# Seven block products of half size for most of w13 in a two-layer decoder trunk

## The chip, the cores and the metric

One core of a Trainium2 chip runs the whole trunk in one program. The metric is device time in microseconds of that core; lower is better. A run can be told from another of the same kernel to about 0.3%.

## What is computed

A trunk of two layers on 512 positions of width 1024, all in float32. Each layer is a feed-forward network, a token mixer and a second feed-forward network, each with a norm that is modulated by a conditioning vector, so there are four networks:

```python
def swiglu(h, w13, w2):
    a, b = jnp.split(h @ w13, 2, axis=-1)
    return (jax.nn.silu(a) * b) @ w2

x = x + 0.5 * g1[:, None] * swiglu(h, ff_w13[l, 0], ff_w2[l, 0])
```

`w13` is 1024 x 5632 (twice D_FF = 2816), `w2` is 2816 x 1024. The mixers (a gated convolution with latent attention in layer 0, sparse attention in layer 1) are not touched. The vectors of the modulation come from `silu(c) @ ada_w`.

## The kernel before

Features lie on the 128 partitions and the 512 positions in the columns. `x` and `h` are eight k-tiles of 128 x 512; `h` is held as a rounded high part and the rest (`hi`, `lo`), and so is each weight. `split` makes the two: ACT copies (L102), DVE subtracts (L103). A product is three matmul passes (`mm3`, L141 to L143): high by high, high by rest, rest by high.

`wunit` (L134) takes a raw weight tile from a ring (`wr`), loads 128-column units of up to eight k-tiles (512 KB) on SP's queue, and splits it into `wh` and `wl`. Each of the three rings has three tiles and one more inside a network (`more_weights`).

`ffn` goes over 22 column blocks `j` (D_FF / 128). A block multiplies `h` by the columns of `a` and of `b`, 24 matmuls of 512 columns each, and `gate` makes `silu(a) * b` and splits it into `g[j]`. The first blocks are made otherwise: in the first network `start` makes three while the first norm is taken; in the others `halves` makes two in two column halves (256 columns), beside the end of the norm before it. Then `proj_out` goes over the eight output blocks `d`: 22 k-tiles of `w2` times `g`, the residual added to `x` (L517), and squares for the next norm. Its last `d` is computed in two column halves, so that the norm of the first half starts early; `norm` hands in instructions through `inject`.

`background` loads `ada_w` in 128 tiles of 512 KB into the same `wr` ring and sums them on DVE (L300 to L304); `step` puts in so many tiles. It is called `st1` times per block `j` and `st2` times per unit of `proj_out`, in three of the networks.

The tile framework allocates buffers of a pool by tag: an instruction that needs a buffer waits for the last reader of the one before. Each engine, and each engine's DMA queue, works in order.

Of the kernel before, what the change touches and what calls it, by code (L numbers as in the profile page):

```python
# [1 line left out]

# [7 lines left out]
F32 = mybir.dt.float32  # L10
# [20 lines left out]
class Net:  # L31
# [6 lines left out]
    def __init__(self, tc, ctx, a):  # L38
# [70 lines left out]
    def wtile(self, kind, dt=R):  # L109

        counts = [n for _, n in self.wsets]
# [11 lines left out]
    def more_weights(self, ctx, name, n):  # L123

        self.wsets.append((ctx.enter_context(self.scratch(name)), n))
        ctx.callback(self.wsets.pop)
# [11 lines left out]
    def mm3(self, out, lhs, rhs, first, last):  # L138
        mm = self.nc.tensor.matmul
# [152 lines left out]
    def background(self, order):  # L292

        due = None
        for l, v in order:
            acc = self.t.tile([P, D], F32, name="acc", tag="acc", bufs=1)
            for k in range(KD):
# [7 lines left out]
                if k == 2 and due:  # L305
                    self.ada(*due)
# [94 lines left out]
    def modulate(self, l, n, d, bc, sl=slice(0, S)):  # L401
# [7 lines left out]
        sh = self.shift(l, n, d)  # L409
        nc.scalar.activation(hi[:, sl], u, AF.Identity, bias=sh)  # L410
# [44 lines left out]
    def ffn(self, l, which, nxt, st1, st2):  # L455
# [4 lines left out]
        ctx = ExitStack()  # L460
        g = []
        new = lambda pool, n: g.extend([[pool.tile([P, S], R, name=f"g{q}_{len(g) + k}") for q in range(2)]
                                        for k in range(n)])

        def gate(j, ab):
# [4 lines left out]
            self.split(gv, *g[j])  # L470

        with ctx:
            if l == 0 and which == 0:
                new(ctx.enter_context(self.scratch("ffa")), 11)
                ab = self.start(0, 0, w13)
                new(ctx.enter_context(self.scratch("ffb")), 11)
                self.more_weights(ctx, "ffw0", 1)
                done = 3
            else:
                new(ctx.enter_context(self.scratch(f"ff{l}{which}")), NJ)  # L480
                self.more_weights(ctx, f"ffw{l}{which}", 1)
# [790 lines left out]
```

## Time and profile before

| | |
|---|---|
| median of 3 runs | 2033.0 us (2030.45 to 2035.76) |
| profiled execution | 2030.4 us, span 2028.7 us |
| busy in the span | PE 1976.1, DVE 1133.6, ACT 767.5, POOL 227.2 us |
| mean granted clock of TensorE | 0.993 of 2.4 GHz |
| moved by DMA | 248.07 MB, mean 122 GB/s |

PE is the matmul engine, PEld its weight loads, which overlap. A matmul's end is modelled, so the distance between the starts of two matmuls says what one costs. Idle time of an engine that is not the bottleneck costs nothing.

### The profile page before, as it was taken

Reading aid. Unit: us, or ns where it says so; the run is one execution under the profiler, and the core shown is the slowest. Engines: PE = TensorE matmul, PEld = TensorE weight load, DVE = VectorE, ACT = ScalarE, POOL = GpSimd, SP = SyncE. Lnnn points to the kernel's source line nnn. Section 1 sums busy time; section 2 is a strip of 40 time slices with the busy share of each in tenths; the row PEclk is TensorE's granted clock in tenths of the full one; section 3 lists DMA queues with packets and bytes.
Section 4 is the critical chain, followed back from the end, with each engine's and each line's share of the span. In section 5 each row is a group of like instructions: output and inputs, shape, how many; then the busy total and the mean of one; then the engine's idle time right before and its main releaser. Section 6 shows DMA issues by size and latency. Waiting matters only on the chain.

```text
span 2028.7 us, 26175 instructions
## 1 busy us (share of the span) xinstructions
PE 1976.1 (97%) x10050; PEld 1669.5 (82%) x10050; DVE 1133.6 (56%) x1917; ACT 767.5 (38%) x1380; POOL 227.2 (11%) x468
## 2 busy tenths in 40 slices
PE   6999999998999999999999999999999999999998
PEld 5788878886889888888988888899788888888887
DVE  7746556358756666564545443356788763333332
ACT  3322222246734222222323222236777743322223
POOL 3000000024400000000100000020555410000000
PEclk8999999999999999999999999999999999999999
DMA  9646657332134566674436442333000134333331
GB/s 280 199 142 189 189 165 224 93 90 72 42 95 124 183 202 199 195 213 118 121 102 193 126 146 90 103 81 102 11 12 17 32 103 116 94 94 96 92 97 49
DMA packets 374562, 248.07 MB, mean 122 GB/s; under 512 B 23335, under 2 KB 356390, under 8 KB 374438
## 3 DMA queue, kind: packets, MB, share of 16 engines
q1 hardware_dynamic: 373568, 245.24, 41.0%
q8 instruction: 79, 1.29, 0.3%
q10 hardware_dynamic: 870, 1.16, 0.2%
q14 instruction: 45, 0.37, 0.1%
HBM read 244.28 MB, written 2.10 MB: 121 GB/s over the span
## 4 chain that ended last, share of the span: by engine, by line
PE 77%; DVE 8%; DMA 5%; ACT 4%; POOL 2%; issue 2%; DVEq 0%; SPq 0%; ACTq 0%; POOLq 0%
PE psA L141 17%; PE psA L143 16%; PE psA L142 16%; PE psY L141 7%; PE psY L143 7%; PE psY L142 7%; DMA wr<-in_ff_w 4%; PE psY L595 2%; DVE acc L236 1%; DVE wl L103 1%; ACT wh L102 1%; PE psA L561 1%; DVE pt L103 1%; ACT e L567 1%; PE psA L586 1%
## 5 line engine op out<-in xcount | busy, mean ns | idle before, releaser
L102 ACT ACTIVATE wh<-wr 128x1024 fp32r<-128x1024 f32 (+2 forms) x325 | 328.3, 1015 | 890.0 <-PE psA L142 317.3
L103 DVE TENSOR_TENSOR wl<-wr,wh 128x1024 fp32r<-128x1024 f32 (+2 forms) x325 | 381.5, 1179 | 414.2 <-ACT wh L102 408.7
L141 PE MATMUL psA<-h,wh 128*128 128x512 f32 (+1 forms) x1312 | 492.8, 379 | 7.5 <-ACT h L410 3.6
L143 PE MATMUL psA<-h,wl 128*128 128x512 f32 (+1 forms) x1312 | 490.2, 374 | 0.0
L142 PE MATMUL psA<-h,wh 128*128 128x512 f32 (+1 forms) x1312 | 487.9, 372 | 1.1 <-DVE h L411 1.0
L141 PEld LDWEIGHTS psA<-h,wh 128*128 128x128 f32 x1312 | 247.5, 189 | 48.4 <-ACT h L410 4.5
L142 PEld LDWEIGHTS psA<-h,wh 128*128 128x128 f32 x1312 | 247.9, 189 | 45.0 <-DVE h L411 2.4
L143 PEld LDWEIGHTS psA<-h,wl 128*128 128x128 f32 x1312 | 247.7, 189 | 43.7
L141 PE MATMUL psY<-h,wh 128*128 128x512 f32 (+2 forms) x568 | 209.0, 369 | 0.3 <-ACT wh L102 0.3
L143 PE MATMUL psY<-h,wl 128*128 128x512 f32 (+2 forms) x568 | 208.7, 367 | 0.0
L142 PE MATMUL psY<-h,wh 128*128 128x512 f32 (+2 forms) x568 | 207.7, 366 | 0.0
L141 PE MATMUL psA<-g,wh 128*128 128x512 f32 (+1 forms) x528 | 192.8, 365 | 0.0
L142 PE MATMUL psA<-g,wh 128*128 128x512 f32 (+1 forms) x528 | 191.9, 363 | 0.0
L143 PE MATMUL psA<-g,wl 128*128 128x512 f32 (+1 forms) x528 | 191.8, 363 | 0.0
L304 DVE SCALAR_TENSOR_TENSOR acc<-wr,cact,acc 128x1024 f32<-128x1024 f32 x112 | 143.7, 1283 | 59.6 <-DMA wr<-in_ada_w 58.2
L376 POOL TENSOR_SCALAR s<-s 128x2 int32<-128x2 int32 (+1 forms) x14 | 5.9, 420 | 1517.4 <-ACT s L375 1517.4
L142 PEld LDWEIGHTS psY<-h,wh 128*128 128x128 f32 (+1 forms) x568 | 106.1, 187 | 18.7
L141 PEld LDWEIGHTS psY<-h,wh 128*128 128x128 f32 (+1 forms) x568 | 106.1, 187 | 18.1 <-ACT wh L102 0.7
L143 PEld LDWEIGHTS psY<-h,wl 128*128 128x128 f32 (+1 forms) x568 | 106.0, 187 | 18.0
L143 PEld LDWEIGHTS psA<-g,wl 128*128 128x128 f32 x528 | 99.6, 189 | 16.0 <-DVE wl L103 0.6
L142 PEld LDWEIGHTS psA<-g,wh 128*128 128x128 f32 x528 | 99.7, 189 | 15.5
L141 PEld LDWEIGHTS psA<-g,wh 128*128 128x128 f32 x528 | 99.7, 189 | 15.4
(274 smaller groups left out, 2615.2 us busy)
## 6 DMA issues: line engine op xcount, KB each, us to landing
wr<-in_ff_w SPq DMA_DIRECT2D x234, 512.0 KB, 3.9
wr<-in_ada_w SPq DMA_DIRECT2D x128, 512.0 KB, 4.3
wr<-in_ff_w SPq DMA_DIRECT2D x40, 384.0 KB, 3.1
ar<-in_ada_w SPq DMA_DIRECT2D x16, 512.0 KB, 6.4
wr<-in_hy_w_in SPq DMA_DIRECT2D x15, 512.0 KB, 3.7
wr<-in_nsa_w_in SPq DMA_DIRECT2D x14, 512.0 KB, 3.7
wr<-in_hy_w_out SPq DMA_DIRECT2D x8, 512.0 KB, 3.6
wr<-in_nsa_w_out SPq DMA_DIRECT2D x16, 256.0 KB, 2.8
```

The costliest lines, as they stand in the source:

```text
L102: nc.scalar.activation(hi, src, AF.Copy)
L103: (lo_eng or nc.vector).tensor_tensor(lo, src, hi.bitcast(F32), op=OP.subtract)
L141: mm(out, lh, rh, start=first, stop=False)
L142: mm(out, lh, rl, start=False, stop=False)
L143: self.product = mm(out, ll, rh, start=False, stop=last).ins
L236: nc.vector.scalar_tensor_tensor(a, r, c, a, op0=OP.mult, op1=OP.add)
L304: nc.vector.scalar_tensor_tensor(acc, raw, self.cact[:, k:k + 1], acc, op0=OP.mult, op1=OP.add)
L376: pool.tensor_scalar(y.bitcast(I32), ms.bitcast(I32), -0.5, float(0x5F3759DF), op0=OP.mult, op1=OP.add)
L561: nc.tensor.matmul(s[:, :w], q[:, i * P:(i + 1) * P], k[:, :w], start=(p == 0), stop=(p == len(u["qk"]) - 1))
L567: nc.scalar.activation(e, e, AF.Exp, bias=mn, scale=-1.0, accum_out=L["sum"][:, i:i + 1])
L586: nc.tensor.transpose(b[:, kb * P:(kb + 1) * P], e[:, kb * P:(kb + 1) * P], self.ident)
L595: nc.tensor.matmul(y[:, kb * P:], u["v"](kb), t[:, 4 * kb:3 * kb + 4, :], start=(first and kb == 0 and p == 0), stop=(u["last"] and kb == ...
```

## The change

Blocks 3 to 21 of three networks, and blocks 11 to 21 of the first, go through a new class `Strassen`. A block is seen as a 2 x 2 product: the columns of `a` and of `b` by the two halves of the 1024 input features, times those halves by the two halves of the positions. Seven products of half size (four k-tiles, three passes, 256 columns: 12 matmuls each) take the place of eight. The sums of `h` that stand on the right (`t1` to `t4`) are made once per network by `right`, from full-precision halves (`keep`, written by `modulate`). The sums of weights that stand on the left are made per block: `x` is the `a` unit; `y` holds, in its lower half, a sum that a load from SP and an adding load from POOL (`accum_op`) make, in its upper half `sum2` of DVE; `v` is the `b` unit with `a`'s upper rows added by an adding load; `w` is `sum4`. `blocks` interleaves the products of block `q` with those of `p` before it and the preparation of `r` after it. Products share a bank that is opened again, and `snap` (ACT) takes its contents in between.

`g` holds 11 blocks at a time: `ffn` makes 11, runs `proj_out` over the first 11 k-tiles of `w2` and adds to `x`, makes the other 11 in the same tiles, and runs `proj_out` again. `w2`'s last three k-tiles are loaded for two `d` at once (384 KB). The `wh` and `wl` rings have five tiles, `wr` still four. The background's steps move (last lines).

```diff
-        self.wsets = [(self.w, 3)]
+        self.wsets = [(self.w, {"wr": 3, "wh": 3, "wl": 3})]
         self.nw = {"wr": 0, "wh": 0, "wl": 0}
+        self.keep = None
...
+    def more_weights(self, ctx, name, nr, n):
+        self.wsets.append((ctx.enter_context(self.scratch(name)), {"wr": nr, "wh": n, "wl": n}))
...
+        if self.keep is not None and sl == HALVES[1]:
+            nc.scalar.activation(self.keep[:, d], u, AF.Identity, bias=sh)
+            self.split(self.keep[:, d], hi[:, sl], lo[:, sl])
+            return
+        if self.keep is not None and sl == slice(0, S):
+            nc.scalar.activation(self.keep[:, d], u[:, HALVES[1]], AF.Identity, bias=sh)
...
+            self.more_weights(ctx, f"ffw{l}{which}", 1, 2)
+            st = Strassen(self, ctx.enter_context(self.scratch(f"ffs{l}{which}")), w13)
+            if not first:
                 b = self.halves([unit(j, q) for j in range(2) for q in range(2)])
                 ab = [b[0:2], b[2:4]]
                 done = 2
+            us = [unit(done, q) for q in range(2)]
             for j in range(done):
-                gate(j, ab[j])
-            for j in range(done, NJ):
+                gated(j, ab[j])
+            st.right()
+            for j in range(done, NH if first else done + 1):
                 ab = []
-                for q in range(2):
+                for u in us or [unit(j, q) for q in range(2)]:
                     b = self.ffbank()
-                    self.gemm(b, unit(j, q), self.hks)
+                    self.gemm(b, u, self.hks)
                     ab.append(b)
-                gate(j, ab)
+                us = None
+                if j == NH - 4:
+                    late_g()
+                gated(j, ab)
                 self.step(st1)
+                done = j + 1
+            if not first:
+                late_g()
+                st.blocks(range(done, NH), g, done)
+            else:
+                st.right_late()
             assert (l, 2 + 6 * which, 0) in self.have
-            self.proj_out(w2, g, self.half[:, l, which, :], nxt, st2)
-    def proj_out(self, w, act, gate, nxt, st=0):
+            self.proj_out(w2[:NH * P], [(q[:, 0], q[:, 1]) for q in g], gate, None, st2[0],
+                          lambda: st.begin(NH))
+            new_g()
+            late_g()
+            st.blocks(range(NH, NJ), g, 0)
+            self.proj_out(w2[NH * P:], [(q[:, 0], q[:, 1]) for q in g], gate, nxt, st2[1])
...
+        tail = {4: 6, 8: 3, 11: 2}[nk] if nxt else 0
+        if nxt:
+            self.begin_norm()
...
+            if before_end and d == KD - 2:
+                before_end()
+            for k0, u in self.proj_units(w, nk, d):
+                self.gemm(b, u, act, k0 == 0, k0 + u[0].shape[1] >= nk, k0=k0)
+            if not nxt or d < KD - 2:
+                self.step(st)
...
+    def __init__(self, net, pool, w13):
+        self.net, self.nc, self.pool, self.w13 = net, net.nc, pool, w13
+        self.t = pool.tile([P, 3, 4, 2, 256], R, name="tq")
...
+    def right(self):
+        net, nc = self.net, self.nc
+        b12, b22 = net.keep[:, 0:4], net.keep[:, 4:8]
+        f32 = lambda half, low: net.h[:, low * KD + 4 * half:low * KD + 4 * half + 4, self.H0].bitcast(F32)
+        new = lambda: net.raw().rearrange("p (k t) -> p k t", k=4)
+        parts = lambda i: (self.t[:, i, :, 0, :], self.t[:, i, :, 1, :])
+        t1, t2, t3 = new(), new(), new()
+        nc.vector.tensor_tensor(t1, f32(0, 0), b12, op=OP.subtract)
+        nc.vector.tensor_tensor(t1, t1, f32(0, 1), op=OP.add)
+        net.split(t1, *parts(0))
+        nc.vector.scalar_tensor_tensor(t2, b22, -1.0, t1, op0=OP.mult, op1=OP.subtract)
+        net.split(t2, *parts(1))
+        nc.vector.tensor_tensor(t3, b22, b12, op=OP.subtract)
+        net.split(t3, *parts(2))
+        t4 = new()
+        nc.vector.scalar_tensor_tensor(t4, t2, -1.0, f32(1, 0), op0=OP.mult, op1=OP.subtract)
+        nc.vector.tensor_tensor(t4, t4, f32(1, 1), op=OP.subtract)
+        self.late = t4
...
+    def load(self, j):
+        net, nc = self.net, self.nc
+        rows = lambda half, q: self.w13[half * S:(half + 1) * S, q * DFF + j * P:q * DFF + (j + 1) * P].rearrange(
+            "(k p) m -> p k m", p=P)
+        whole = lambda q: self.w13[:, q * DFF + j * P:q * DFF + (j + 1) * P].rearrange("(k p) m -> p k m", p=P)
+        new = lambda: net.raw().rearrange("p (k m) -> p k m", k=KD)
+        x, y, v = new(), new(), new()
+        nc.sync.dma_start(x, whole(0))
+        nc.sync.dma_start(y[:, 0:4], rows(0, 1))
+        nc.gpsimd.dma_start(y[:, 0:4], rows(1, 1), accum_op=OP.add)
+        nc.sync.dma_start(v, whole(1))
+        nc.gpsimd.dma_start(v[:, 0:4], rows(0, 0), accum_op=OP.add)
+        self.ready[j] = dict(j=j, xr=x, yr=y, vr=v)
+        return self.ready[j]
+    def parts(self, u, name, raw):
+        net = self.net
+        hi, lo = (net.wtile(k).rearrange("p (k m) -> p k m", k=KD) for k in ("wh", "wl"))
+        u[name] = hi, lo
+        net.nc.scalar.activation(hi, raw, AF.Copy)
+        return lambda: net.nc.vector.tensor_tensor(lo, raw, hi.bitcast(F32), op=OP.subtract)
+    def sum2(self, u):
+        self.nc.vector.tensor_tensor(u["yr"][:, 4:8], u["yr"][:, 0:4], u["xr"][:, 0:4], op=OP.add)
+    def sum4(self, u):
+        nc = self.nc
+        u["wr"] = self.net.tmp("s4").rearrange("p (k m) -> p k m", k=4)
+        nc.vector.tensor_tensor(u["wr"], u["yr"][:, 4:8], u["xr"][:, 4:8], op=OP.add)
+        hi, lo = (self.pool.tile([P, 4, P], R, name=n, tag=n, bufs=2) for n in ("s4h", "s4l"))
+        nc.scalar.activation(hi, u["wr"], AF.Copy)
+        u["w"] = hi, lo
+        return lambda: nc.vector.tensor_tensor(lo, u["wr"], hi.bitcast(F32), op=OP.subtract)
+    def product(self, out, left, k0, right, first):
+        hi, lo = left
+        for kk in range(4):
+            self.net.mm3(out, (hi[:, k0 + kk, :], lo[:, k0 + kk, :]), right[kk], first and kk == 0, kk == 3,
+                          not first)
+    def snap(self, tag, src, bufs):
+        t = self.pool.tile([P, 256], F32, name=tag, tag=tag, bufs=bufs)
+        self.nc.scalar.activation(t, src, AF.Copy)
+        return t
+    def begin(self, j):
+        u = self.load(j)
+        lo = self.parts(u, "x", u["xr"])
+        lo()
+        self.sum2(u)
+        lo = self.parts(u, "y", u["yr"])
+        lo()
+        lo = self.sum4(u)
+        lo()
+    def finish(self, u, g):
+        nc = self.nc
+        gv = u["gv"]
+        nc.vector.scalar_tensor_tensor(gv[:, self.H1], u["c"], -1.0, u["b"], op0=OP.mult, op1=OP.mult)
+        self.net.split(gv, g[:, 0], g[:, 1])
+    def blocks(self, js, g, g0):
+        nc, net = self.nc, self.net
+        js = list(js)
+        if js[0] not in self.ready:
+            self.begin(js[0])
+        p = o = None
+        for n in range(len(js) + 1):
+            q = self.ready.get(js[n]) if n < len(js) else None
+            r = self.load(js[n + 1]) if n + 1 < len(js) else None
+            if o:
+                self.finish(o, g[g0 + n - 2])
+            if p:
+                self.product(p["A"], p["v"], 0, self.t3, False)
+                p["c"] = self.snap("sc", p["A"], 1)
+                nc.vector.tensor_tensor(p["c"], p["c"], p["Q"], op=OP.add)
+            if q:
+                lo = self.parts(q, "v", q["vr"])
+                lo()
+                q["A"] = net.bank()[:, 0:256]
+                self.product(q["A"], q["x"], 0, self.b11, True)
+                q["a"] = self.snap("sa", q["A"], 2)
+            if r:
+                self.sum2(r)
+                lo_x = self.parts(r, "x", r["xr"])
+                lo_y = self.parts(r, "y", r["yr"])
+            if q:
+                Y = net.bank("Y")[:, 0:256]
+                self.product(Y, q["x"], 4, self.b21, True)
+                nc.vector.tensor_tensor(q["a"], q["a"], Y, op=OP.add)
+                nc.scalar.activation(q["a"], q["a"], AF.Silu)
+            if r:
+                lo_x()
+            if q:
+                self.right_late()
+            if p:
+                self.product(p["A"], p["v"], 4, self.t4, False)
+                p["gv"] = net.tmp("gv")
+                nc.vector.scalar_tensor_tensor(p["gv"][:, self.H0], p["A"], -1.0, p["a"], op0=OP.mult, op1=OP.mult)
+            if r:
+                lo_y()
+            if q:
+                self.product(q["A"], q["y"], 4, self.t2, False)
+                q["b"] = self.snap("sb", q["A"], 2)
+            if r:
+                lo_w = self.sum4(r)
+            if p:
+                self.product(p["Q"], p["w"], 0, self.b22, False)
+                nc.vector.tensor_tensor(p["b"], p["b"], p["Q"], op=OP.add)
+                nc.scalar.activation(p["b"], p["b"], AF.Silu)
+            if r:
+                lo_w()
+            if q:
+                q["Q"] = net.bank()[:, 0:256]
+                self.product(q["Q"], q["y"], 0, self.t1, True)
+            o, p = p, q
+        self.finish(o, g[g0 + len(js) - 1])
...
+        n.ffn(0, 0, n.ffn_room(0, 0), norm(0, 1), 3, (3, 3))
         n.mixer0(norm(0, 2))
-        n.ffn(0, 1, norm(1, 0), 2, 1)
-        n.ffn(1, 0, norm(1, 1), 1, 1)
+        n.ffn(0, 1, n.ffn_room(0, 1), norm(1, 0), 0, (3, 3))
+        n.ffn(1, 0, n.ffn_room(1, 0), norm(1, 1), 0, (2, 2))
         n.mixer1(norm(1, 2))
-        n.ffn(1, 1, lambda hf: n.final(out, hf), 0, 0)
+        n.ffn(1, 1, n.ffn_room(1, 1), lambda hf: n.final(out, hf), 0, (0, 0))
```

## Rows read from the trace of the kernel before

**Rows 1.** The page: totals of engines, and GB/s in 40 slices.
```profile
PE 1976.1 (97%) x10050; PEld 1669.5 (82%) x10050; DVE 1133.6 (56%) x1917; ACT 767.5 (38%) x1380; POOL 227.2 (11%) x468
...
GB/s 280 199 142 189 189 165 224 93 90 72 42 95 124 183 202 199 195 213 118 121 102 193 126 146 90 103 81 102 11 12 17 32 103 116 94 94 96 92 97 49
```
**Rows 2.** Busy time by stretch: the start, then two networks.
```profile
core 0: us, PE busy (x) PEld busy (x) DVE busy (x) ACT busy (x) POOL busy (x), PEclk, DMA share, GB/s
0.00:70.00 70.00, 52.01 (x240) 42.51 (x241) 57.25 (x115) 22.74 (x35) 20.28 (x27) 0.90 0.82 238
...
820.00:970.00 150.00, 150.00 (x699) 125.47 (x698) 78.87 (x96) 35.93 (x44) 0.00 (x0) 1.00 0.55 166
...
1700.00:1870.00 170.00, 170.00 (x744) 139.49 (x743) 57.45 (x61) 48.87 (x62) 0.00 (x0) 1.00 0.33 96
```
**Rows 3.** Timeline of PE, 512 columns: start, us; 45 matmuls apart.
```profile
700.99 0.39 PE L141 MATMUL psA<-h,wh 128*128 128x512 f32 x1
...
711.29 0.39 PE L141 MATMUL psA<-h,wh 128*128 128x512 f32 x1
```
**Rows 4.** SP's waits (total, times, longest); two pieces of the chain.
```profile
SPq L134 <- DVE wl L103: 1030.8, 243, 31.1
...
225.55 1.14 DVE wl L103
226.74 4.82 DMA wr<-in_ff_w
```
**Rows 5.** Timeline of PE, 256 columns, in two places.
```profile
592.78 0.28 PE L141 MATMUL psY<-h,wh 128*128 128x256 f32 x1
...
602.55 0.28 PE L143 MATMUL psY<-h,wl 128*128 128x256 f32 x1
...
967.73 0.28 PE L143 MATMUL psY<-g,wl 128*128 128x256 f32 x1
...
970.25 0.28 PE L143 MATMUL psA<-g,wl 128*128 128x256 f32 x1
```
**Rows 6.** Groups of DVE by shape: busy us, mean ns; idle before.
```profile
L103 DVE TENSOR_TENSOR wl<-wr,wh 128x1024 fp32r<-128x1024 f32 x276 | 339.2, 1233 | 335.0 <-ACT wh L102 329.6
L304 DVE SCALAR_TENSOR_TENSOR acc<-wr,cact,acc 128x1024 f32<-128x1024 f32 x112 | 143.7, 1283 | 59.6 <-DMA wr<-in_ada_w 58.2
L103 DVE TENSOR_TENSOR g<-gv,g 128x512 fp32r<-128x512 f32 x88 | 60.1, 683 | 14.8 <-ACT g L102 14.8
L103 DVE TENSOR_TENSOR wl<-wr,wh 128x768 fp32r<-128x768 f32 x32 | 30.6, 956 | 79.2 <-ACT wh L102 79.2
L354 DVE TENSOR_TENSOR nacc<-nacc,sq 128x512 f32<-128x512 f32 x32 | 22.0, 687 | 5.1 <-ACT sq L349 4.9
L311 DVE STREAM_TRANSPOSE tr<-acc 128x512 f32<-128x512 f32 x32 | 20.7, 686 | 0.0
L312 DVE TENSOR_REDUCE s<-tr 128x16 f32<-128x512 f32 x32 | 20.3, 676 | 0.0
L103 DVE TENSOR_TENSOR pt<-psA,pt 128x256 fp32r<-128x256 f32 x40 | 16.5, 413 | 0.6 <-ACT pt L102 0.5
L517 DVE SCALAR_TENSOR_TENSOR x<-psA,half,x 128x512 f32<-128x512 f32 x18 | 13.5, 751 | 31.5 <-PE psA L143 31.4
L517 DVE SCALAR_TENSOR_TENSOR x<-psA,mod,x 128x256 f32<-128x256 f32 x8 | 3.9, 482 | 3.1 <-PE psA L143 3.1
```
**Rows 7.** Groups of ACT by shape.
```profile
L102 ACT ACTIVATE wh<-wr 128x1024 fp32r<-128x1024 f32 x276 | 291.1, 1058 | 775.4 <-DMA wr<-in_ff_w 265.9 <-PE psA L142 242.1 <-issue 149.3
L102 ACT ACTIVATE g<-gv 128x512 fp32r<-128x512 f32 x88 | 55.5, 630 | 42.5 <-DVE gv L469 42.2
L410 ACT ACTIVATE h<-u,mod 128x256 fp32r<-128x256 f32 x80 | 35.3, 499 | 49.0 <-DVE u L406 49.0
L102 ACT ACTIVATE pt<-psA 128x256 fp32r<-128x256 f32 x40 | 15.1, 377 | 2.6 <-PE psA L586 2.4
```
**Rows 8.** DMA issues, median us to landing: whole span, whole span, 1870 to 2008.
```profile
ar<-in_ada_w SPq DMA_DIRECT2D x16, 512.0 KB, 6.4
...
wr<-in_nsa_w_out SPq DMA_DIRECT2D x16, 256.0 KB, 2.8
...
wr<-in_ff_w SPq DMA_DIRECT2D x14, 512.0 KB, 3.5
```
**Rows 9.** One group of POOL.
```profile
L279 POOL TENSOR_TENSOR wl<-wr,wh 128x768 fp32r<-128x768 f32 x8 | 16.6, 2078 | 28.3 <-ACT wh L278 28.3
```

More of the change, by code (lines that the diff above doesn't have):

```diff
@@ L1 @@
 from contextlib import ExitStack
+from functools import partial
 import numpy as np
@@ L136, in wunit, with mm3 @@
         return hi, lo
-    def mm3(self, out, lhs, rhs, first, last):
-        mm = self.nc.tensor.matmul
+    def mm3(self, out, lhs, rhs, first, last, reopen=False):
+        mm = partial(self.nc.tensor.matmul, skip_group_check=True) if reopen else self.nc.tensor.matmul
         (lh, ll), (rh, rl) = lhs, rhs
@@ L453, in halves, with ffn_room, ffn @@
         return banks
-    def ffn(self, l, which, nxt, st1, st2):
+    def ffn_room(self, l, which):
+        ctx = ExitStack()
+        pool = ctx.enter_context(self.scratch(f"ffg{l}{which}"))
+        self.keep = pool.tile([P, KD, 256], F32, name="keep", tag="gx")
+        return ctx, pool
+    def ffn(self, l, which, room, nxt, st1, st2):
         nc = self.nc
@@ L459, in ffn, with new_g, late_g, gated @@
         unit = lambda j, q: self.wunit(w13[:, q * DFF + j * P:q * DFF + (j + 1) * P], KD, P)
-        ctx = ExitStack()
+        ctx, pool = room
+        NH = NJ // 2
+        gate = self.half[:, l, which, :]
         g = []
-        new = lambda pool, n: g.extend([[pool.tile([P, S], R, name=f"g{q}_{len(g) + k}") for q in range(2)]
-                                        for k in range(n)])
-        def gate(j, ab):
+        def new_g():
+            g[:] = [pool.tile([P, 2, S], R, name=f"g{j}", tag=f"g{j}") for j in range(NH - 2)]
+        def late_g():
+            gx = pool.tile([P, 2, 2, S], R, name="gx", tag="gx")
+            g.extend(gx[:, j] for j in range(2))
+        def gated(j, ab):
             s = self.tmp("silu")
@@ L504, in proj_out @@
+    def proj_out(self, w, act, gate, nxt, st=0, before_end=None):
         nc = self.nc
         nk = len(act)
-        tail = 1 if nk > KD else 3
-        units = lambda d: [(k0, self.wunit(w[k0 * P:min(k0 + KD, nk) * P, d * P:(d + 1) * P],
-                                           min(KD, nk - k0), P)) for k0 in range(0, nk, KD)]
-        self.begin_norm()
-        def products(b, us, sl=slice(0, S)):
-            for k0, u in us:
-                self.gemm(b, u, act, k0 == 0, k0 + KD >= nk, sl, k0)
+        tail = {4: 6, 8: 3, 11: 2}[nk] if nxt else 0
+        if nxt:
+            self.begin_norm()
@@ L1220, in final, with quarter, right_late @@
         yield
+class Strassen:
+    H0, H1 = slice(0, 256), slice(256, 512)
+    def __init__(self, net, pool, w13):
+        self.net, self.nc, self.pool, self.w13 = net, net.nc, pool, w13
+        self.t = pool.tile([P, 3, 4, 2, 256], R, name="tq")
+        self.late = None
+        self.ready = {}
+    def quarter(self, half, sl):
+        h = self.net.h
+        return [(h[:, 4 * half + kk, sl], h[:, KD + 4 * half + kk, sl]) for kk in range(4)]
+    def right(self):
[16 more added lines that the diff above has]
+        self.late = t4
+        net.keep = None
+        tq = lambda i: [(self.t[:, i, kk, 0, :], self.t[:, i, kk, 1, :]) for kk in range(4)]
+        self.b11, self.b21, self.b22 = self.quarter(0, self.H0), self.quarter(1, self.H0), self.quarter(1, self.H1)
+        self.t1, self.t2, self.t3, self.t4 = tq(0), tq(1), tq(2), self.quarter(0, self.H1)
+    def right_late(self):
+        if self.late is not None:
+            h = self.net.h
+            self.net.split(self.late, h[:, 0:4, self.H1], h[:, KD:KD + 4, self.H1])
+            self.late = None
+    def load(self, j):
[107 more added lines that the diff above has]
+        self.finish(o, g[g0 + len(js) - 1])
+        self.ready.clear()
```

48 lines of the change are left out of this document (26 added, 22 removed).

## The prediction

> **What bounds the kernel now.** I read the engine totals of the page first. TensorE (PE) is busy 1976.1 of 2028.7 us [rows 1], and in two stretches inside feed-forward networks it is busy for the whole stretch, while VectorE (DVE) has 57.45 and ScalarE (ACT) 48.87 of 170 us, GpSimd (POOL) nothing, at granted clock 1.00 (2.4 GHz) [rows 2]. Next the timeline of PE alone, since a modelled busy time overlaps the next one: what a matmul costs is the distance between starts. From 700.99 to 711.29 us there are 45 matmuls of 512 columns, 0.2289 us each [rows 3]. So the matmuls bound the kernel there, and fewer streamed columns shorten it, if everything else keeps up. The waits of the sync engine's (SP's) queue show that weight loads stand ready and wait for a free buffer: 243 waits, 1030.8 us, on the pass that last reads `wr` [rows 4]. That slack exists at 48 long matmuls per block; the change takes from it.
>
> **What PE gains.** A block `j` is 48 matmuls now: 48 x 0.2289 = 10.99 us. In Strassen's scheme it is seven products of four k-tiles by three passes, 84 matmuls of 256 columns. The trace has such matmuls, each with its own weight load: 592.78 to 602.55 us is 83 of them, 0.1177 apart; 967.73 to 970.25 us is 21, 0.1200 apart [rows 5]. That makes 9.89 to 10.08 us per block; I take 9.89. Blocks changed: 11 in the first network, 8 + 11 in each of the three others, 68. If PE stayed the bound, the gain would be 68 x 1.10 = 75 us.
>
> **What a block then asks of the others.** DVE per block, in durations of [rows 6]: three rests of 1024 columns (1.233 each), `sum2`, `sum4` and the rest of the fourth sum (512 columns, 0.687 each), the rest of `g` (0.683), three additions of 256 columns with a PSUM operand (0.413 each), two gate products (0.482 and about that): 3.70 + 2.06 + 0.68 + 1.24 + 0.96 = 8.6 us of 9.89. Before it was two rests, one product, one rest of `g`: 3.8 of 10.99. ACT: three copies of 1.058, two of 0.630, five of 0.377 [rows 7]: 6.3 us. Both fit, DVE with little room. ACT's three snapshots each have two other products, 2.8 us, between them and the next writer of their bank, so they cost PE nothing unless ACT's queue is held up.
>
> **The loop that I expect to decide.** There are four `wr` buffers and a block takes three (`x`, `y`, `v`). Those of `x` and `y` are free only after `sum4` of their block. So the `y` of the block after next can be loaded only then, in two transfers, one behind the other: SP loads 256 KB, and when it has landed POOL issues the adding load into the same bytes. Then `sum2`, which stands in DVE's queue ahead of everything that leads to the next `sum4`. Behind a waiting `sum2` DVE holds the addition that makes the silu's input, so ACT's silu and the snapshot `b` behind it, which PE's first product of the next iteration needs. The period of this loop:
> - DVE from `sum2` to `sum4` in the order written: 0.687 + 0.413 + 1.233 + 0.482 + 1.233 + 0.687 = 4.74 us. ACT's high part of `y` and the silu fit beside it.
> - First load: the 256 KB rows say 2.8 us from issue to landing [rows 8].
> - Adding load: no row of before shows one, nor any transfer issued by POOL. It moves 256 KB from HBM, reads 256 KB of SBUF as well, and its issue is POOL's. Lower end: a plain 256 KB load, 2.8 us. Upper end: the slowest median of a 512 KB load, 6.4 us [rows 8]. I take 3.5, a 512 KB load in a quiet stretch [rows 8], as it is nearest in bytes.
> - Signals between the four steps: about 0.15 us, 0.05 from the end of a `wl` pass to the load that waited for it [rows 4].
>
> Sum 4.74 + 2.8 + 3.5 + 0.15 = 11.19 us, above the 9.89 of PE and above the 10.99 of before. With the ends it is 10.5 to 14.1. The point of no gain is an adding load of 3.3 us. The `v` buffers have a whole iteration more and don't bind.
>
> The Trainium skill (DMA: Bandwidth & Descriptors, section on the anatomy of a DMA issued by GpSimd) fits such a transfer, without an addition, with 2.0 us plus bytes over 436 GB/s: 2.6 us here, an estimate. No run here shows it yet; our own 256 KB and 512 KB rows (2.8 and 3.5) have the same form with a smaller slope. By it the period would be 10.3 us and the whole sum below about zero, 2032.
>
> The loop rules between blocks, not for the first of each of seven calls of `blocks`: 61 x (11.19 - 10.99) = +12 us, and 7 x (9.89 - 10.99) = -8 us.
>
> **Other parts.**
> - `right()`: on DVE seven passes of 1.233 and two of 1.283 [rows 6], 11.2 us, queued behind the gating of block 1 (about 2 us) and ahead of the gating of block 2 and of the first `x` rest (1.4 + 1.23). In three networks only one block of 10.99 us covers it: 2 + 11.2 + 2.6 = 15.8, so PE is late by about 5. The four temporaries take all `wr` buffers, so the first `y` starts its two transfers about 12 us in and its rest is done at about 21, 3 us after PE would want it. I take 8 us per network, 24 together, between 0 (DVE's order lets it start beside the 11 us of `halves`) and 15 each. In the first network eight plain blocks cover it.
> - Background: 128 steps move into the projections, three per `d` in 28 of them. One `d` is 33 x 0.2289 = 7.55 us on PE and loads 512 + 192 + 1536 KB = 2.29 MB. At the highest mean that a slice of the page shows, 280 GB/s [rows 1], that takes 8.2 us: 28 x 0.65 = 18 us. Ends: 0, and 59 at the 238 GB/s of the first 70 us [rows 2]. DVE has 1.23 + 0.48 + 3 x 1.28 + 1.02 + 0.75 = 7.3 us per `d` [rows 6] (half a pair's rest, three steps, three eighths of the four transposes and sums at a vector's end, the residual), no cover left.
> - Ends of the seven calls: three products that wait on one another's snapshots, about 1 us each, 7; the last `g` (about 2.7 us) is hidden by the 24 matmuls of k-tiles 0 to 7 of the next projection, 5.5 us.
> - `keep`: one more ACT pass per `d` (0.499 [rows 7], eight per network) beside the first half of `halves` (96 x 0.1177 = 11.3 us): nothing, 4 us each if uncovered. The second residual addition (0.75 on DVE, eight per network) lies beside 7.5 us of matmuls. The longer tail in the attention's projection: under 1 us.
>
> **Sum** against the profiled execution (2030.4 us, span 2028.7): +12 - 8 + 24 + 18 + 7 = +53, so 2083; the median of the runs shown is 2.6 above that execution, so 2086.
>
> **Rivals.**
> 1. *The loop does not bind.* If the tile framework places DVE's instructions otherwise, with only the four passes that read the two buffers in the loop (0.69 + 1.23 + 1.23 + 0.69 = 3.84) and the adding load near its lower end, the period is 3.84 + 2.8 + 2.8 + 0.15 = 9.6, below PE's 9.89. Then 68 x 1.10 = -75, with +24 + 18 + 7 still paid: 2007; 1983 if the starts are covered too, 1965 with the background besides. For it: DVE's sum fits, and the 256 KB rows are steady at 2.8. Against it: every block has two transfers in series, which none has now. This is the faster side.
> 2. *An adding load costs no more than a plain one* (its lower end): the period is 10.49, and 61 x (-0.50) - 8 + 49 = +11, 2044; at 2.6 us for the load it would be 2032, no change. The fit of the page named above speaks for it, the second operand against it.
> 3. *The adding load is dear*: near or above its upper end, because an addition in the transfer or POOL's making of it (512 rows of 512 bytes) is slow. At 5.5 us the period is 13.2: 61 x 2.2 = 134 - 8 + 49, 2208. It decides from about 4.5 us (2147). For it: POOL's ordinary instructions are the slowest of all engines in the rows that compare (2.08 us for 768 columns against DVE's 0.96 [rows 6, 9]). Against it: transfers are not POOL's arithmetic.
> 4. *Strassen's matmuls don't run at 0.118* because each product ends in another bank and reopens it. At 0.131 a block is 10.99 and nothing is gained even at PE. Against it: in `halves` and the projections' tails banks change as often [rows 5].
>
> **How the numbers follow.** Forecast (period 10.6 to 12.2, 2050 to 2145): 0.44. Rival 1: 0.33. Rival 2: 0.09 (2025 to 2050; 0.03 each of faster, same and slower). Rival 3: 0.12. Rival 4: 0.02. What a measurement of this kernel tells from no change is 0.3%, 6 us. Faster 0.33 + 0.03 = 0.36; same 0.05 with the edges of the cases beside it; slower 0.59. The forecast alone spans 2050 to 2145; the range reaches into rivals 1 and 3 until a tenth is left out at each side: 1982 to 2165.
>
> **What would show it.** In the changed profile: starts of 256-column matmuls 0.118 to 0.120 apart inside a product (if not, the gain is wrong); PE idle about 1.3 us per iteration, released by ACT's snapshot or a rest on DVE, which waits for `sum2`, which waits for the adding load (if PE has no idle there, rival 1); landing of the adding load near 3.5 us (over 4.5: rival 3); PE idle of some 8 us after block 2 of three networks; DMA at 280 GB/s or more in the first halves of the projections of the first two networks. The prediction is wrong if the period between equal products is under 10.5 us, or if the starts cost nothing.

## The result and the profile after

The changed kernel takes 2285.2 us (median of 4 runs, 2281.0 to 2288.0), the kernel before beside it 2032.9 (4 runs, 2030.5 to 2035.8): a ratio of 1.124, 95% interval 1.122 to 1.126. Slower was forecast, 2086 and at most 2165; the time lies 120 us above the range.

The page of the changed kernel: totals of engines against [rows 1], the granted clock in 40 slices, and the two large DMA queues. `q0` holds POOL's loads; the kernel before has no such queue.

```profile
PE 2019.0 (88%) x12534; PEld 1818.9 (80%) x12534; DVE 1477.5 (65%) x2543; ACT 970.5 (42%) x1839; POOL 400.8 (18%) x604
...
PEclk8989898999999899999899999999999999999999
...
q1 hardware_dynamic: 395072, 263.07, 39.5%
q0 software_dynamic: 71808, 35.66, 12.8%
```

No engine is busy for 97% of the span any more. A stretch of the last call of `blocks` (columns as in [rows 2], where PE was busy for 170.00 of 170 us at clock 1.00):

```profile
2084.00:2140.00 56.00, 45.67 (x350) 44.85 (x349) 32.83 (x51) 25.20 (x45) 10.29 (x8) 0.93 0.66 138
```

So PE stands 10 us of 56, and DVE has room as well. What they wait for shows in the waits of all engines and of SP's queue (total, times, longest), and in one group of DVE and one of ACT (columns of [rows 6]):

```profile
DVE wr L1363 <- DMA wr<-in_ff_w: 265.9, 66, 9.9
...
SPq L1348 <- DVE s L1369: 355.5, 39, 13.7
```
```profile
L1363 DVE TENSOR_TENSOR wr<-wr 128x512 f32<-128x512 f32 x68 | 47.1, 692 | 272.7 <-DMA wr<-in_ff_w 265.9 <-issue 6.8
...
L1359 ACT ACTIVATE wh<-wr 128x1024 fp32r<-128x1024 f32 x204 | 213.6, 1053 | 395.6 <-DVE wr L1363 199.9 <-DMA wr<-in_ff_w 114.2 <-PE psA L145 30.7
```

`sum2` (L1363) stands for 4 us in each of 66 blocks until a load has landed; SP's first load of `y` (L1348) waits for `sum4` (L1369) 39 times. In [rows 4] SP waited for passes on `wl`, and its loads stood ready. One period of the loop, from the timelines of DVE, SP, POOL, ACT and PE (start, duration, idle before and what ended it):

```profile
2109.39 0.68 DVE L1369 TENSOR_TENSOR s<-wr 128x512 f32<-128x512 f32 x1
...
2110.13 0.37 SPq L1348 DMA_DIRECT2D wr<-in_ff_w  x1
2110.59 0.46 SPq L1350 DMA_DIRECT2D wr<-in_ff_w  x1
...
2113.81 1.28 POOL L1349 DMA_DIRECT2D wr<-in_ff_w  x1 [10.05 <-ACT sc L1383]
...
2118.76 0.69 DVE L1363 TENSOR_TENSOR wr<-wr 128x512 f32<-128x512 f32 x1 [3.63 <-DMA wr<-in_ff_w]
...
2121.84 0.36 ACT L1383 ACTIVATE sb<-psA 128x256 f32<-128x256 f32 x1
...
2122.19 0.68 DVE L1369 TENSOR_TENSOR s<-wr 128x512 f32<-128x512 f32 x1
...
2122.26 0.39 PE L143 MATMUL psA<-tq,wh 128*128 128x256 f32 x1 [2.50 <-ACT sb L1383]
```

From `sum4` to `y`'s load 0.74 us, to the adding load 3.68, to `sum2` 4.95, to the next `sum4` 3.43: 12.80, where eight whole products took 10.99. It is one of the shorter periods: over the 56 that are under 20 us the medians are 3.63 for the first load, 5.60 for the adding load, 3.43 from `sum2` to `sum4`, and 13.0 in all. The DMA issues (median us to landing, against [rows 8]):

```profile
wr<-in_ff_w POOLq DMA_DIRECT2D x136, 256.0 KB, 5.0
wr<-in_ff_w SPq DMA_DIRECT2D x68, 256.0 KB, 3.0
```

And PE's timeline of the iteration before, against [rows 5]:

```profile
2097.73 0.58 PE L143 MATMUL psA<-tq,wh 128*128 128x256 f32 x1 [4.39 <-ACT sb L1383]
2098.11 0.42 PE L144 MATMUL psA<-tq,wh 128*128 128x256 f32 x1
2098.33 0.41 PE L145 MATMUL psA<-tq,wl 128*128 128x256 f32 x1
...
2100.89 0.33 PE L145 MATMUL psA<-h,wl 128*128 128x256 f32 x1
2101.06 0.28 PE L143 MATMUL psA<-h,wh 128*128 128x256 f32 x1
...
2103.53 0.28 PE L143 MATMUL psA<-h,wh 128*128 128x256 f32 x1
```

From 2101.06 to 2103.53 are 21 matmuls, 0.1176 apart, as forecast. After the idle 4.39 us they are 0.213 apart until 2100.89: the lower level, 1.2 GHz.

By PE's timeline the seven calls of `blocks` (first product to projection) take 13.50, 14.30, 13.87, 14.47, 13.53, 13.47 and 12.77 us per block: 928 us in all, 181 more than 68 x 10.99. The other 71 of the 252 lie outside the blocks.

### The profile page after: what moved, and what is told of

It is laid out like the page before. It is cut to its first block, busy times and chain, and to the rows that moved or that the text cites. A ratio compares the mean times of both kernels' runs of the same rounds, so it can differ in the third digit from the quotient of the medians.

```text
span 2284.1 us, 33037 instructions
## 1 busy us (share of the span) xinstructions
PE 2019.0 (88%) x12534; PEld 1818.9 (80%) x12534; DVE 1477.5 (65%) x2543; ACT 970.5 (42%) x1839; POOL 400.8 (18%) x604
## 3 DMA queue, kind: packets, MB, share of 16 engines
q0 software_dynamic: 71808, 35.66, 12.8%
## 5 line engine op out<-in xcount | busy, mean ns | idle before, releaser
L143 PE MATMUL psA<-h,wh 128*128 128x256 f32 (+1 forms) x1144 | 381.1, 337 | 52.3 <-ACT sc L1383 22.8
L1359 ACT ACTIVATE wh<-wr 128x1024 fp32r<-128x1024 f32 x204 | 213.6, 1053 | 395.6 <-DVE wr L1363 199.9
L144 PE MATMUL psA<-h,wh 128*128 128x256 f32 (+1 forms) x1144 | 372.7, 326 | 1.2 <-DVE h L419 1.0
L145 PE MATMUL psA<-h,wl 128*128 128x256 f32 (+1 forms) x1144 | 372.0, 325 | 0.7 <-DVE wl L105 0.7
L143 PE MATMUL psA<-tq,wh 128*128 128x256 f32 x816 | 251.8, 309 | 134.1 <-ACT sb L1383 112.5
L104 ACT ACTIVATE wh<-wr 128x1024 fp32r<-128x1024 f32 (+2 forms) x185 | 184.1, 1000 | 356.7 <-DMA wr<-in_ff_w 197.8
L1360 DVE TENSOR_TENSOR wl<-wr,wh 128x1024 fp32r<-128x1024 f32 x204 | 248.5, 1223 | 105.2 <-ACT wh L1359 104.7
L105 DVE TENSOR_TENSOR wl<-wr,wh 128x1024 fp32r<-128x1024 f32 (+2 forms) x185 | 214.6, 1167 | 147.7 <-ACT wh L104 146.7
L143 PEld LDWEIGHTS psA<-tq,wh 128*128 128x128 f32 x816 | 169.2, 207 | 145.6 <-ACT sb L1383 122.8
L1349 POOL DMA_DIRECT2D wr<-in_ff_w x68 | 89.3, 1313 | 899.3 <-DMA wr<-in_ff_w 242.5
L145 PE MATMUL psA<-tq,wl 128*128 128x256 f32 x816 | 245.9, 302 | 0.8 <-DVE wl L1360 0.8
L144 PE MATMUL psA<-tq,wh 128*128 128x256 f32 x816 | 244.8, 300 | 0.0
L1363 DVE TENSOR_TENSOR wr<-wr 128x512 f32<-128x512 f32 x68 | 47.1, 692 | 272.7 <-DMA wr<-in_ff_w 265.9
L145 PEld LDWEIGHTS psA<-tq,wl 128*128 128x128 f32 x816 | 170.3, 209 | 1.0 <-DVE wl L1360 1.0
L144 PEld LDWEIGHTS psA<-tq,wh 128*128 128x128 f32 x816 | 170.1, 208 | 0.0
```

Of the source, the lines that this page charges most:

```text
L104: nc.scalar.activation(hi, src, AF.Copy)
L105: (lo_eng or nc.vector).tensor_tensor(lo, src, hi.bitcast(F32), op=OP.subtract)
L143: mm(out, lh, rh, start=first, stop=False)
L144: mm(out, lh, rl, start=False, stop=False)
L145: self.product = mm(out, ll, rh, start=False, stop=last).ins
L1349: nc.gpsimd.dma_start(y[:, 0:4], rows(1, 1), accum_op=OP.add)
```

## The experiments

Theory 1: the loop through `y`'s two loads sets the period. Theory 2: TensorE, its clock or the mere number of transfers does. Times below are of a single run unless a number of runs is given. The kernel before took 2038.1 beside `noadd`, `ring6`, `plain` and `plain_steps`, 2031.6 beside `nov`, `noy`, `ring6o` and `poolsum`; 17 runs of it lie between 2029.8 and 2038.8, so differences of a few us between single runs say little. Times per block are PE's, from the first product of a call to the projection.

**Without the adding loads.** The two `accum_op` lines are deleted, so the sums that they make are left out.

> Changed kernel without the two adding loads of each block (y's lower half is then one weight block, v is the plain b unit; block products come out wrong). Ring of four tiles as in the changed kernel. Theory 1 (latency of the adding load in the loop): period 4.1 + 0.1 + 3.0 = 7.2 to 7.9 us, under the 9.9 of PE, so blocks at 10.0 to 10.3 and total about 2045 to 2060. Theory 2 (DVE, ACT and the clock): blocks stay above 12.5, total above 2200. If this one gains and the larger ring does not, it is POOL's or the DMA engines' throughput on adding loads.

Measured 2058.4, and 10.38 us per block. The adding loads cost 3.27 us per block, 222 of the 252 us; without them seven products beat eight, by 0.6 of the 1.10 us that PE could give. A stretch of that kernel's last call:

```profile
1894.00:1954.00 60.00, 60.00 (x507) 60.00 (x507) 47.30 (x74) 36.85 (x61) 0.00 (x0) 1.00 0.46 130
```

**One of the two.** `nov` drops `v`'s line, `noy` drops `y`'s.

```diff
-        nc.gpsimd.dma_start(v[:, 0:4], rows(0, 0), accum_op=OP.add)
```

> The changed kernel without the adding load into v (its values are wrong there); y's adding load stays. Theory 1 (a loop: the y buffer is free after sum4, then SP's load of y, then its adding load, then sum2 to sum4; v stands outside it): a block stays near 13 us, what is saved is y's wait behind v in POOL's queue, up to 1.3 us x 68 = 90: 2195 to 2260. Theory 2 (any adding load costs by what it takes of DMA engines and POOL, wherever it stands): half of the 227 that both together cost, 2170. Below 2150 theory 1 falls.

> The changed kernel without the adding load into y (its values are wrong there); v's stays, which lands in about 5 us like y's but is wanted an iteration later. Theory 1 (loop): the loop loses 5.0 us and more, a block takes 10.4 to 11 us as without both: 2058 to 2100. Theory 2 (cost by engines' time, wherever): half of the 227, 2170. Over 2140 theory 1 falls.

Measured 2226.8 (12.84 per block) and 2153.9 (11.78). `nov` lies where theory 1 put it. `noy` is above the 2140 at which I said that theory 1 falls, in the form in which `v` stands outside the loop: alone `y`'s adding load costs 2.46 us per block and `v`'s 1.40. With four buffers for three tiles `v`, too, is loaded into a buffer that a `sum4` frees. The trace of `noy` shows that this binds: in 60 of 68 blocks ACT's copy of `v` starts within 0.25 us of the landing of `v`'s adding load, and behind that copy stand in ACT's queue the silu and the snapshot for which PE waits. Here the load landed 4.4 us after its issue:

```profile
2032.01 1.28 POOL L1350 DMA_DIRECT2D wr<-in_ff_w  x1 [13.77 <-DVE sc L1418]
...
2036.56 1.06 ACT L1358 ACTIVATE wh<-wr 128x1024 fp32r<-128x1024 f32 x1 [5.70 <-PE psA L144]
...
2039.19 0.39 PE L143 MATMUL psA<-tq,wh 128*128 128x256 f32 x1 [2.59 <-ACT sb L1382]
```

(The view names PE for ACT's wait, as the matmul's modelled end lies 0.08 us behind the landing.) In the changed kernel `v`'s (L1351) besides goes ahead of the `y` of its own block in 6 of 68 cases:

```profile
332.25 1.28 POOL L1351 DMA_DIRECT2D wr<-in_ff_w  x1 [10.49 <-DMA wr<-in_ff_w]
333.47 1.37 POOL L1349 DMA_DIRECT2D wr<-in_ff_w  x1
...
338.90 0.69 DVE L1363 TENSOR_TENSOR wr<-wr 128x512 f32<-128x512 f32 x1 [5.12 <-DMA wr<-in_ff_w]
```

**The same loads without the addition.**

```diff
-        nc.gpsimd.dma_start(y[:, 0:4], rows(1, 1), accum_op=OP.add)
+        nc.gpsimd.dma_start(y[:, 0:4], rows(1, 1))
```

> The changed kernel with the two loads by POOL as plain loads that overwrite instead of adding (the sums are left out, its values are wrong); same queue, same bytes, same order and waits. Which part of the 5.0 us is the addition? Theory A (the addition in the transfer is dear): POOL's loads land in 2.8 to 3.2 us like SP's of 256 KB, the loop shortens by about 2 us, 61 x 2: 2130 to 2180. Theory B (POOL's making of the transfer, 1.3 us on the engine and what follows, is dear, not the addition): they land in 4.5 to 5.0 us, 2250 to 2285.

Measured 2193.9, 12.36 per block. The queue and the landing of this kernel:

```profile
q0 software_dynamic: 10880, 35.66, 5.4%
...
wr<-in_ff_w POOLq DMA_DIRECT2D x136, 256.0 KB, 3.6
```

Between the numbers of both theories. Over `y` and `v` together POOL's path costs 0.6 us over SP's 3.0, the addition 1.4 more. For `y`, which stands in the loop, it is otherwise (L1349 in the changed kernel, then here):

```profile
DMA to landing us min/median/max: 4.4/5.2/7.5
```
```profile
DMA to landing us min/median/max: 3.2/4.3/6.2
```

For `y` the addition is 0.9, and POOL's load without it already 1.3 over SP's. `v`'s went from 4.8 to 3.4. `y`'s runs beside the 512 KB loads of `v` and of the next `x`, which SP issued 0.46 and 1.10 us behind `y`'s first load in the period above. No run takes these away, so that they are the reason is not shown. The addition moves the same 35.66 MB in 71808 packets instead of 10880, and takes the DMA engines 2.5 times as long (12.8% of 2284 against 5.4% of 2192 us). Of the 91 us saved 88 lie in the blocks, 1.29 each. Without any addition the kernel is still 161 us slower than before.

**Six load buffers, and the order on DVE.**

```diff
-            self.more_weights(ctx, f"ffw{l}{which}", 1, 2)
+            self.more_weights(ctx, f"ffw{l}{which}", 3, 2)
```

> Changed kernel with six raw weight tiles instead of four inside the networks, and nothing else in the block loop. To make room the third right-hand sum shares the place of the second, so block products come out wrong; the work is the same. Theory 1 (loop: a block's y tile can be loaded only when the block before has been summed, then plain load 3.0 us, adding load 5.0 us, 4.1 to 4.7 us of DVE): with two more tiles the y of the next block is loaded an iteration earlier, the loop goes, blocks fall from 13.65 us to 10.0 to 10.5, total 2285 - 68 x 3.3 = about 2060. Theory 2 (the blocks are bound by DVE's and ACT's queues and the clock that drops after each gap, whatever the ring): under 60 us gained, above 2225. Theory 3 (the DMA engines or POOL's making of adding loads is the bound, throughput and not latency): no gain, same 13.6 us per block.

Measured 2181.3, 12.60 per block, between the numbers of the theories: most of the loop was left. 72 of the 104 us gained lie in the blocks. Its DVE timeline says why:

```profile
909.85 0.68 DVE L1369 TENSOR_TENSOR s<-wr 128x512 f32<-128x512 f32 x1
...
922.13 0.69 DVE L1363 TENSOR_TENSOR wr<-wr 128x512 f32<-128x512 f32 x1 [6.54 <-DMA wr<-in_ff_w]
...
924.54 0.68 DVE L1369 TENSOR_TENSOR s<-wr 128x512 f32<-128x512 f32 x1
...
935.38 0.69 DVE L1363 TENSOR_TENSOR wr<-wr 128x512 f32<-128x512 f32 x1 [5.10 <-DMA wr<-in_ff_w]
```

The framework had put `sum2` of the next block ahead of `sum4` of this one. So `sum4`, which frees the buffer, waited for the next adding load after all: 14.7 us from one `sum4` to the next. `ring6o` changes that order only:

```diff
-        self.nc.vector.tensor_tensor(u["yr"][:, 4:8], u["yr"][:, 0:4], u["xr"][:, 0:4], op=OP.add)
+        with (self.net.tc.issue_after(self.last4) if self.last4 is not None else ExitStack()):
+            self.nc.vector.tensor_tensor(u["yr"][:, 4:8], u["yr"][:, 0:4], u["xr"][:, 0:4], op=OP.add)
...
-        nc.vector.tensor_tensor(u["wr"], u["yr"][:, 4:8], u["xr"][:, 4:8], op=OP.add)
+        self.last4 = nc.vector.tensor_tensor(u["wr"], u["yr"][:, 4:8], u["xr"][:, 4:8], op=OP.add).ins
```

> Six load buffers instead of four as in ring6 (t3 takes the place of t2, so its values are wrong), and sum2 held in DVE's queue behind the sum4 of the block before. In ring6 sum2 of a block stood ahead of the sum4 before it (s2 922.13, s4 924.54 us), so that the sum4 that frees y waited for y's next adding load all the same: one iteration, 14.5 us. Theory 1 (loop, closed by that order): now it runs over two iterations, (about 13 from sum4 to sum2 and 8 from there to sum4) / 2, so 10.5 to 11.2 us per block and 2060 to 2110. Rival (the adding loads themselves are too many for the queue, two of 5 us one behind the other per block): stays at 12.6 per block, 2181.

Measured 2103.6, 11.45 per block and 10.31 in the last call, with every adding load still there (median 5.3 us to landing). Theory 1 holds: a load of 5 us is cheap where two periods hide it. The transfers are as many as in the changed kernel, so their number did not set the period. 1.07 us per block over the 10.38 without adding loads stay, and no run separates them.

**Work for the idle TensorE.** 24 matmuls ahead of the first product of 61 iterations; their result goes nowhere.

> The changed kernel with 24 more matmuls of 256 columns (their result is thrown away) ahead of the first product of 61 iterations: 24 x 0.118 = 2.8 us more of TensorE each, 173 us in all. Theory 1 (loop over loads and DVE): TensorE waits there anyway, the time stays, 2285 +- 25. Rival (TensorE or its clock is what a block costs, 13.2 us of 88% busy): up to 2450.

Measured 2307.4: 22 us for 173 us of matmuls. In this stretch PE now never stands, and the clock is full:

```profile
2110.00:2170.00 60.00, 60.00 (x508) 60.00 (x507) 34.48 (x54) 26.82 (x46) 11.88 (x10) 1.00 0.68 132
```

So the lost clock (0.947 over the changed kernel, 0.993 before, 0.972 here) followed from the idle time. With most of it back the blocks are no shorter, 13.97 us against 13.65, and with 2.8 us more of matmuls each no more than 0.32 longer: neither TensorE nor its clock sets the period, and theory 2 falls.

**Plain blocks in the new frame.** `plain` keeps `g` in halves, the cut projections and the moved steps, with whole products of 512 columns; `plain_steps` also puts the steps back.

```diff
-            st.right()
...
-            st.blocks(range(NH, NJ), g, 0)
+            plain(range(NH, NJ), NH)
```

> Changed kernel with plain blocks in place of Strassen's (24 + 24 matmuls of 512 columns), everything else of the change kept: g in two halves, two projections, w2's tail units shared by two output blocks, background steps where the change puts them, rings. The right-hand sums and the kept copy of h fall away. From the stages of the two traces, blocks of Strassen cost +181 us, projections +37, the first network's plain blocks +26, gaps at norms +10. Theory 1: what is left is the cost of the moved background steps: 2033 + 37 + 10 + 10 to 20 = 2090 to 2105. Rival: the projections' and plain blocks' loss is a consequence of the Strassen parts (sums of h on DVE, late g, clock): 2035 to 2060.

> The same plain blocks, with the background steps about where they were before (2 per block and 1 to 2 per output block of the projections in the first two networks, 1 and 1 in the third). Theory 1 (the loss outside the blocks is the crowding of three steps per output block): back to 2033 within 15 us. Rival (two half projections, shared units of w2 and a second addition to x cost by themselves): stays above 2060.

Measured 2084.8 and 2058.6. The moved steps of `plain` cost 26 us, the rest of the frame 20, give or take the few us between single runs. The eleven plain blocks of the first network's second half, where three steps went into each (`plain`), and the same with two (`plain_steps`):

```profile
237.20:386.40 149.20, 129.85 (x536) 104.20 (x535) 90.72 (x111) 34.76 (x44) 0.00 (x0) 0.91 0.64 193
```
```profile
224.30:345.40 121.10, 121.10 (x532) 99.42 (x531) 71.23 (x84) 33.61 (x42) 0.00 (x0) 1.00 0.59 177
```

In the first DMA brings 193 GB/s and PE waits for weights; in the second PE is full. These 28 us hold all of the 26, and the changed kernel does not have them: its seven-product blocks call no `step`. So the 26 are not the price of its moved steps. In the 20 of the frame, 5.06 us is one wait between two networks, for the weights of the first product with `h`, which the kernel before does not have.

**The sums on POOL.** All of them follow from `x` and `v`, so no load into `y` is needed.

```diff
-        nc.sync.dma_start(y[:, 0:4], rows(0, 1))
-        nc.gpsimd.dma_start(y[:, 0:4], rows(1, 1), accum_op=OP.add)
         nc.sync.dma_start(v, whole(1))
-        nc.gpsimd.dma_start(v[:, 0:4], rows(0, 0), accum_op=OP.add)
+        nc.gpsimd.tensor_tensor(y[:, 0:4], v[:, 0:4], v[:, 4:8], op=OP.add)
+        nc.gpsimd.tensor_tensor(v[:, 0:4], v[:, 0:4], x[:, 0:4], op=OP.add)
```

> No adding loads and no loads into y: y's lower half is the sum of v's two halves and v's lower half gets x's lower half added, both by POOL from loaded buffers (two 128x512 additions, some 1.3 us each), which needs 1024 KB per block instead of 1792. Theory 1: as without adding loads, 10.2 to 10.6 us per block: 2045 to 2075. Rival: POOL's additions are slow or slow DVE down beside them, so that DVE (8.6 us per block) passes 10 us: 2090 or more.

> As poolsum, but y's two halves lie in working tiles of their own, so that the four load buffers go to x and v alone: the buffer that v is loaded into is that of two blocks before, and no load waits for sum4. In poolsum a chain sum4 (2009.68) to v's load (2010.42) to POOL's addition (2014.47) to sum2 (2016.28) to sum4 (2019.63) was left. Theory 1: with it gone 10.0 to 10.3 us per block as without adding loads (10.12): 2045 to 2070. Rival (POOL's additions, 1.3 to 1.8 us each, are what costs 10.8 in poolsum): 2105 to 2120.

Measured 2113.8 (11.17 per block) and, with `y` in working tiles so that no load waits for `sum4`, 2073.1 (10.78). Of the 0.79 us over 10.38 the loop was half; the other half stays, and POOL's additions beside DVE are the likely reason, which no run shows alone. POOL's and DVE's timelines of `poolsum`:

```profile
2002.76 1.30 POOL L1349 TENSOR_TENSOR wr<-wr 128x512 f32<-128x512 f32 x1 [7.45 <-DVE gv L1400]
2004.14 1.81 POOL L1350 TENSOR_TENSOR wr<-wr 128x512 f32<-128x512 f32 x1
...
2004.70 2.32 DVE L1359 TENSOR_TENSOR wl<-wr,wh 128x1024 fp32r<-128x1024 f32 x1
```

Side by side POOL's addition takes 1.81 instead of 1.30 us and DVE's rest 2.32 instead of 1.23.

**Seven products in the second layer only.** `hybrid2`: the first layer's networks as before, the second layer's with the sums of `ytmp`. `hybrid3`: there two plain blocks ahead of the seven-product ones instead of one, and the third network's steps moved (1 in each plain block; 2 and 1 in its projections).

> The two networks of the first layer as in the kernel before (eight-size products, one projection, background steps in the blocks), those of the second layer by seven products with the sums of ytmp. Theory 1: 38 blocks at 10.15 instead of 10.99, -32, and some +12 for the starts, the right sides and the cut projections of two networks: 2005 to 2025. Rival (the structure costs as much as it did in the plain kernels, 10 and more per network, and the blocks stay at 10.8): 2030 to 2050.

> As hybrid2, but two plain blocks instead of one cover the right sides' VectorE work in the networks of the second layer (seven products for 7 + 11 blocks there, 36 in all), and the background steps of the third network lie 1 in each plain block, 2 and 1 in its projections. In hybrid2 TensorE waited 6 us in the last network's first call and 6.6 at the start of the third network's second. If these starts are what eats the blocks' gain: 2035 - 6 - 6 = 2023 to 2030. If not, 2032 to 2037.

`hybrid2`: 2035.0 (12 runs) against 2034.1 (17), ratio 1.000, interval 0.999 to 1.002. It lies in the rival's range: the 11-block call of the last network runs at 10.23 per block, the other three at 11.1, above the 10.99 of whole products. `hybrid3`: 2023.2 (5 runs, 2020.4 to 2024.7) against 2031.7 (9 runs), ratio 0.9956, interval 0.9940 to 0.9971: 0.4% faster than the kernel before, inside the range that was expected. PE's waits from 1680 to 1960 us, in `hybrid2` and in `hybrid3`:

```profile
PE psA L143 <- ACT sc L1476: 3.2, 1, 3.2
PE psA L143 <- ACT sb L1476: 2.9, 2, 1.7
```
```profile
PE psA L143 <- ACT sb L1476: 2.3, 2, 1.4
PE psA L143 <- ACT sc L1476: 1.5, 1, 1.5
```

The waits of the last network shrink from 7.4 to 4.2 us in all. By PE's timeline, from the first product with `h` to the last of the projection, that network goes from 370.6 us (before) over 365.6 to 361.9. The reason that was expected holds only there. The third network, up to the first product with `h` of the mixer behind it, is 2.7 us longer than before in `hybrid2` and 6.6 in `hybrid3`, and PE still stands 5.1 us in the first blocks of its second call (6.6 in `hybrid2`). So from `hybrid2` to `hybrid3` these two networks cancel. Of the 6.6 us between the two profiled executions 6 lie in one stretch of the second mixer, whose code is the same, `hybrid2` first:

```profile
1396.00:1437.00 41.00, 37.02 (x165) 30.58 (x164) 20.33 (x46) 19.00 (x49) 6.90 (x14) 0.88 0.28 74
```
```profile
1399.80:1434.30 34.50, 32.21 (x164) 26.92 (x162) 20.37 (x46) 18.90 (x49) 6.72 (x14) 1.00 0.31 88
```

The granted clock is 0.88 there in one and 1.00 in the other. How often that falls on either kernel no trace shows, so how much of the 12 us between them the starts gave stays open, and the hit of the expected range is in part luck.

## Why the prediction was wrong

- **TensorE's gain** (0.118 per matmul): right. Rival 4 is out.
- **The loop**: the mechanism was right, place by place, and rival 1 is out: PE's idle time ends at the snapshot, behind `sum2`, behind the adding load. Three of its four terms were mis-sized, in the period shown above: the first load 3.68 to POOL's issue instead of 2.8 (the 512 KB of `v` are issued 0.46 us behind it), the adding load 4.95 instead of 3.5, DVE 4.11 instead of 4.74 (one rest of 1.22 us stands behind `sum4`, and DVE waits 0.93 for ACT's copy). The sum is 12.80 instead of 11.19.
- **The step that failed** is the price of the adding load, 3.5 us as "nearest in bytes" to a 512 KB load. `y`'s took 5.2 to landing. This is rival 3, which I gave 0.12: it was to decide from 4.5 us and to give 2147 there, 2208 at 5.5; the measured time lies above both. Two things were left out of the price: the addition (0.9 us for `y`) and that POOL's load in its place takes 4.3 even without it. The fit of the Trainium skill (DMA: Bandwidth & Descriptors, anatomy of a DMA issued by GpSimd) gives 2.6 us, an estimate, and lies below even that plain load; by it the loop would not have mattered. (The prediction reads a smaller slope than the fit's from the rows of 2.8 and 3.5. They give 0.7 us for 256 KB more; the Trainium skill's figure gives 0.6, an estimate.)
- **That step is not all.** With 5.2 for the adding load the prediction's own sum gives a period of 12.89 and 2190, 95 us under what was measured. And `poolload`, whose loads by POOL take the 3.6 that was nearly priced, measured 2193.9, 108 over the forecast. The rest is in the first load above and in the points that follow.
- **"The `v` buffers don't bind"**: wrong. `noy` shows 1.40 us per block for `v`'s adding load alone, and ACT's copy of `v` waiting for it. It doesn't explain why the calls differ: those of `nov`, without it, run from 11.69 to 13.99 us per block.
- **Blocks together**: the prediction's loop, shortened calls, starts and ends come to +35 over 747; measured +181.
- **`right` in the first network** was priced at nothing: "eight plain blocks cover it". They don't. The projection behind them starts at 188.55 us, in `plain`, which has the same blocks and steps up to there but no `right` and no `keep`, at 164.51, and in `ring6` at 172.53. `right`'s four temporaries take all four load buffers, and with six buffers most of the loss is gone. It is 24 of the 71 us outside the blocks. The changed kernel's PE and SP's waits (60 to 190 us), then `plain` and `ring6`:

```profile
163.38 0.79 PE L143 MATMUL psA<-h,wh 128*128 128x512 f32 x1 [9.47 <-ACT wh L104]
...
188.55 0.39 PE L143 MATMUL psA<-g,wh 128*128 128x512 f32 x1
...
SPq L302 <- DVE wr L1320: 16.6, 1, 16.6
```
```profile
164.51 0.50 PE L143 MATMUL psA<-g,wh 128*128 128x512 f32 x1 [0.25 <-ACT wh L104]
```
```profile
172.53 0.40 PE L143 MATMUL psA<-g,wh 128*128 128x512 f32 x1
```

- **Background and frame**: +18 forecast. By PE's timeline the projections of the first two networks, with the norms behind them, take 46 us longer than before. In the first of the two it is 24; `plain`, with the same three steps in each output block, takes 22 longer there, `plain_steps` 6. So in that network the moved steps are about 16 and the cut projections, for which I had charged nothing, about 6. In the second network the two are not separated.
- **Starts**, 24 forecast in the three other networks: in the changed kernel the waits for a first `y` are about 3 us in a network (1178.06, idle 2.73 and 0.78 soon after). That `right` costs 24 in the first network is the same number by luck. Once the loop is gone the starts decide more: in `hybrid2` PE waits 3.2 us in the last network's first call and 6.6 at one start in the third network.
- **Clock**: not priced. It fell to 1.2 GHz after the idle time shown above; `filler` shows that the blocks are no shorter with the clock full, since PE waits anyway.

## What to carry to other kernels

Before two transfers are put in series into one buffer, add up the time from the last reader of the buffer to the next one, and look where the release stands in its engine's order: a buffer more helps only if the release is not queued behind the next load's reader. A scheme that cuts TensorE's work by a tenth must find every sum beside it; here it paid only in the last network of `hybrid2` and `hybrid3`, where the sums had left the loop and no background ran. Temporaries that share a ring with loads belong in the sum too, as `right` shows. An operation that no trace shows is best measured by itself first, when a whole forecast stands on it.

## What the runs showed of the hardware

- An adding load of 256 KB (512-byte rows) took 5.0 us to landing and 1.28 us on POOL, the same load without the addition 3.6 and 0.75, SP's 3.0 (medians over `y` and `v`; `y`'s alone 5.2 and 4.3); the addition raised the packets from 80 to 528 per transfer.
- An addition on POOL and a subtraction on DVE, run together, took 1.81 instead of 1.30 and 2.32 instead of 1.23 us. The Trainium skill (GPSIMD Engine Reference, Specifications) names contention at the SBUF interfaces that the two engines share, when DVE's instruction has two SBUF inputs, as here; the trace agrees.
- After 4.39 us without a matmul 15 matmuls ran at 1.2 GHz, 0.213 us apart, before 0.118 came back.
